# A precedence offset for the small products of scans, sample steps and mixer chunks in a two-layer hybrid trunk

## The chip, the core and the metric

The kernel runs on one core of a Trainium2 chip. The core has engines that run beside each other, each with a queue that it works off in order: TensorE (PE in the profile, with PEld for its weight loads) for products, VectorE (DVE) and ScalarE (ACT) for elementwise work, GpSimd (POOL) for slower elementwise work, and SyncE (SP), from which all large DMA transfers are issued. An instruction waits at the head of its queue for the semaphores of those whose results or buffers it needs. The metric is the device time of one execution in microseconds.

## The reference: one step of a hybrid trunk

1024 prompt tokens and 8 sample tokens go through two layers of width 1024 in fp32. Layer 0 mixes with a Mamba-2 state space scan (SSD, 16 heads) beside an mLSTM (4 heads); layer 1 with RWKV-7 (16 heads of 64). Each mixer is followed by a SwiGLU feed forward of width 2816. For the sample tokens the recurrent states are inputs. The core, cut:

```python
def _trunk(x, conv, ssm, mc, mn, mm, shift, wkv, p):
    for layer in range(DEPTH):
        xn = _rms(x, p['norm_mix'][layer])
        if layer % 2 == 0:
            mix, st = _ssd_mlstm_mixer(xn, conv[i], ssm[i], mc[i], mn[i], mm[i], p, i)
        else:
            mix, st = _rwkv7_mixer(xn, shift[j], wkv[j], p, j)
        x = x + mix.astype(x.dtype)
        x = x + _swiglu(_rms(x, p['norm_ffn'][layer]), p['ffn_w_gate_up'][layer], p['ffn_w_down'][layer])
    y = _rms(x, p['norm_final'])

def _rwkv7_scan(r, decay, k, v, kk, a, s0):
    def step(s, inp):
        r_t, w_t, k_t, v_t, kk_t, a_t = inp
        sa = jnp.einsum('bhvk,bhk->bhv', s, -kk_t)
        s = (s * w_t[:, :, None, :] + sa[..., None] * (kk_t * a_t)[:, :, None, :]
             + v_t[..., None] * k_t[:, :, None, :])
        return s, jnp.einsum('bhvk,bhk->bhv', s, r_t)
```

## The kernel before

**Dense products.** [...] `dense_tile` makes one output tile of 128 rows from 8 or 16 terms into one PSUM bank, `wload` brings 512 KB of weights and splits them on ACT (`whi`, L174) and DVE (`wlo`, L144). Tokens are worked on in two halves (512 prompt tokens; 512 and the 8 sample tokens) from layer 0's output projection on. Dense products are named by their bank: `ps_wo` (RWKV's output projection), `ps_g`, `ps_u` and `ps_d` (the feed forward's gate, up and down products), `ps_rw` (RWKV's projections). `norm_sum` adds squares on DVE (`n_acc`) and sums them over channels by one product (`n_ps`, L211).

**Small products.** The recurrences run beside dense tiles, driven by hooks that advance a generator by a step for each tile of a feed forward or a projection. Beside layer 0's first feed forward half, `ml_decode` steps the mLSTM states of the 8 sample tokens: load `Cs` (L772), update it on DVE (L147), multiply it with the queries (`nums`, L786). The RWKV scan (`rwkv_scan`) runs over the 8 head pairs of a half, numbered 0 to 7; the second half's scan runs beside the end of the second half's projection, the out-projection of the first half and layer 1's feed forward of the first half. For each pair:

- `rw_pre` makes the products `AB` (L1271), four groups of two chunks, and writes the triangular blocks out by DMA;
- `rw_inv` loads them as 32 blocks of 32 x 32 (`X`), sets their diagonals (L1307), inverts them on POOL by 30 dependent pairs of multiply and add (`t`, `X`, L144), writes them (L1317) and loads them into `obd` (L1325), which DVE transposes in blocks (L1327); the first product `off` (L1330) goes through ACT to the second (L1337), whose result goes out by DMA and comes back as `tbd`;
- `rw_front` makes, for each of four groups, the transposes `av` (L1376) and the products `sc`, `Z`, `M` (all issued at L1353), each on a result of the one before that went through DVE;
- `rw_fin` carries the state from chunk to chunk: products `fin` (L1413, L1415), a copy on ACT, a transpose (L1423), a copy on DVE;
- `rw_ln` normalises (`sum2`, L162 and L163, as for `bon` and `kks`); `rw_dec` steps the sample tokens' states (`sav` at L162 and L163, `ysd` at L1533).

The inverse of pair j + 1 is worked on while pair j is scanned.

**What sets the order.** The program is written as one sequence, and a scheduler with a model of the engines' times puts each engine's instructions in the order in which it issues them: among those that are ready by its model, the one of highest precedence, which by default is the earlier one in the program. That order is fixed when the kernel is built; on the chip each queue runs strictly in it. PSUM banks come from pools: three for dense tiles, five or two for the scan's `bank`, two for `pbank`, one for `fin`.

Of the kernel before, what the change touches and what calls it, by code (L numbers as in the profile page):

```python
# [8 lines left out]
F32 = mybir.dt.float32  # L9
# [19 lines left out]
NEG = -1e30  # L29

# [59 lines left out]
def _body(tc, nc, I, O, top):  # L90
# [13 lines left out]
    # two streams of dense products, each with its own weight buffers and banks  # L104
# [28 lines left out]
    ident = cst("ident")  # L133
    S.copy(onesr, cst("onesblk"))
# [24 lines left out]
    def sum2(ps, c, src, hi, lo, e=None):  # L159
        # product with a constant matrix that F32R holds exactly  # L160
        split(src, hi, lo, e)
        PE.matmul(out=ps, lhsT=c, rhs=hi, start=True, stop=False)  # L162
        PE.matmul(out=ps, lhsT=c, rhs=lo, start=False, stop=True)  # L163
# [24 lines left out]
    def dense_tile(w, xs, name, evac, m=128, blocks=NBLK, base=0, th=TA_):  # L188
        # w: list of (hi, lo) per contraction tile; xs: matching (hi, lo) tiles whose column 0 is token base
# [10 lines left out]
    def norm_sum(src, tp, n0, n, w, bank):  # L200
        # Ln of the mean square per token
# [33 lines left out]
    # ------------------------------------------------------------------ layer 0 mixer  # L235
# [37 lines left out]
    # projections with the causal convolution  # L273
# [82 lines left out]
    # gates: rows dt 0..15, i 32..35, f 64..67  # L356
    with gst2:
# [22 lines left out]
        # SSD step sizes and decays  # L380
# [18 lines left out]
        # decode step sizes and decays, per head  # L399
# [11 lines left out]
        # mLSTM row recurrences  # L411
# [25 lines left out]
        # decode gates of the mLSTM  # L437
# [17 lines left out]
    # SSD over chunks  # L455
# [4 lines left out]
    def ssd_chunk(c):  # L460
# [6 lines left out]
        for hf in range(2):  # L467
            b = bank("xT")
            for q in range(4):
                PE.transpose(b[:, q * 128:q * 128 + 128], xc[:, hf * 4 + q, :], ident)  # L470
# [5 lines left out]
        for g in range(2):  # L476
            PE.transpose(b[:, g * 128:g * 128 + 128], bc[:, g, :], ident)
        S.copy(btok, b[:, 0:256])
        xw = sp.tile([128, 1024], F32, name=f"xw{c}", tag="xw", bufs=1)
        for g in range(2):  # L480
# [13 lines left out]
            PE.matmul(out=sc[:, 0:128], lhsT=bc[:, g, :], rhs=bc[:, 2 + g, :], start=True, stop=True)  # L494
            tt(D, D, sc[:, 0:128].unsqueeze(1).to_broadcast([128, 8, 128]))
            yb = bank("yb")
            for q in range(4):
                for h2 in range(2):
                    h = g * 8 + 2 * q + h2
                    PE.matmul(out=yb[h2 * 64:h2 * 64 + 64, q * 128:q * 128 + 128], lhsT=xdt[:, h * 64:h * 64 + 64],  # L500
# [5 lines left out]
            if c > 0:  # L506
                yi = bank("yi")
                for q in range(4):
                    PE.matmul(out=yi[:, q * 128:q * 128 + 128], lhsT=state[g][:, q * 128:q * 128 + 128],
# [12 lines left out]
            PE.matmul(out=su, lhsT=btok[:, g * 128:g * 128 + 128], rhs=xw[:, g * 512:g * 512 + 512],  # L522
# [14 lines left out]
    def ssd_dec_prep():  # L537
# [3 lines left out]
        for i in range(4):  # L541
            PE.transpose(b[0:8, i * 128:i * 128 + 128], bcs[:, i, :], ident)
# [43 lines left out]
    # mLSTM projections  # L586
# [1219 lines left out]
```

## Time and profile before

| | us |
|---|---|
| median of three runs | 3507.38 |
| lowest and highest | 3503.52, 3516.32 |
| span of the profiled execution | 3519.2 |
| TensorE busy in it | 3257.4 (93%) |
| mean granted TensorE clock in it | 0.969 of full speed |

Of the profiled execution the profile has the span, from its first to its last instruction; its time is taken as that. It is 11.8 us above the median of the three timed runs. The profile counts 22615 TensorE instruction records: a small fp32 product makes two of them, one of the dense products one. A view by waits lists, for an engine's instruction, whose end it waited for: total us, times, the longest. A view by windows lists each engine's busy time in a stretch and the clock that TensorE was granted. A row of the timeline has the start, the duration, engine, line, operation, output from inputs, and in brackets how long the engine had sat idle and what ended it. The chain that ended last is followed back from the last instruction to whatever released each step.

### The profile page before, as it was taken

To read this page: it belongs to the slowest core of one execution; us is meant where nothing else is said; L and a number is where in the kernel's file an instruction comes from. 1 tells how busy PE (TensorE), PEld (TensorE's weight loads), DVE (VectorE), ACT (ScalarE), POOL (GpSimd) and SP (SyncE) were. 2 spreads that over 40 slices of the span, in tenths; PEclk is the share of its full clock that TensorE was granted. 3 is DMA by queue.
4 is the path that set the end of the run, shared out by engine and by line. 5 is a ranking of instruction groups with operands and counts; after the bars stand their busy time and mean duration, and the time that the engine had idled before them with its cause. 6 is when DMAs were issued, how large, how long until landed. Compare 5 with 4: busy or idle time off the path is not lost.

```text
span 3519.2 us, 61254 instructions
## 1 busy us (share of the span) xinstructions
PE 3257.4 (93%) x22615; PEld 2997.6 (85%) x22615; DVE 2340.3 (67%) x4315; ACT 1654.6 (47%) x3701; POOL 1237.7 (35%) x1586
## 2 busy tenths in 40 slices
PE   6998899999999999999999968988989999999998
PEld 6987789887778887779999958977888889999998
DVE  8865644466666477676766687667887786575555
ACT  5444435434244245554554555665555554453223
POOL 3257421121200002254645566237686773000000
PEclk9999999999999999999999989998999999999999
DMA  3567674563663243553333324462433333433232
GB/s 117 122 183 215 202 203 143 178 209 126 216 207 108 94 145 109 175 156 93 104 105 97 96 76 134 129 200 76 116 98 98 102 93 90 143 97 97 85 101 68
DMA packets 399135, 458.26 MB, mean 130 GB/s; under 512 B 154756, under 2 KB 295524, under 8 KB 398708
## 3 DMA queue, kind: packets, MB, share of 16 engines
q1 hardware_dynamic: 398836, 454.34, 43.3%
q8 instruction: 179, 2.93, 0.3%
q14 instruction: 120, 0.98, 0.1%
HBM read 352.10 MB, written 102.07 MB: 129 GB/s over the span
## 4 chain that ended last, share of the span: by engine, by line
PE 54%; POOL 13%; DVE 12%; DMA 10%; ACT 5%; issue 4%; SPq 2%; DVEq 0%; ACTq 0%; POOLq 0%
PE ps_g L185 9%; PE ps_u L185 9%; PE ps_d L185 9%; PE ps_rw L185 6%; POOL t L144 5%; POOL X L144 5%; PE ps_in L185 4%; PE ps_out L185 4%; PE ps_o L185 2%; ACT L153 2%; PE ps_wo L185 1%; PE ps_z L185 1%; DVE lp L147 1%; DMA D<-scr_acr 1%; PE cu L726 1%
## 5 line engine op out<-in xcount | busy, mean ns | idle before, releaser
L185 PE MATMUL ps_d<-al,dhi 128*128 128x260 f32 (+2 forms) x1248 | 389.4, 312 | 25.6 <-DVE xc L144 10.3
L185 PE MATMUL ps_d<-ah,dlo 128*128 128x260 f32 (+2 forms) x1248 | 375.6, 301 | 0.0
L185 PE MATMUL ps_d<-ah,dhi 128*128 128x260 f32 (+2 forms) x1248 | 375.3, 301 | 0.0
L144 POOL TENSOR_TENSOR X<-X,t 32x30 f32<-32x30 f32 (+14 forms) x480 | 305.8, 637 | 32.4
L144 POOL TENSOR_TENSOR t<-X 32x30 f32<-32x30 f32 (+14 forms) x480 | 295.5, 616 | 31.0
L185 PEld LDWEIGHTS ps_d<-al,dhi 128*128 128x128 f32 x1248 | 239.4, 192 | 48.3 <-DVE xc L144 15.6
L185 PEld LDWEIGHTS ps_d<-ah,dlo 128*128 128x128 f32 x1248 | 239.8, 192 | 7.9
L185 PEld LDWEIGHTS ps_d<-ah,dhi 128*128 128x128 f32 x1248 | 239.5, 192 | 7.5 <-issue 0.2
L144 DVE TENSOR_TENSOR wlo_g<-raw_g,whi_g 128x512 fp32r<-128x512 f32 (+1 forms) x192 | 143.6, 750 | 113.5 <-ACT whi_g L174 110.8
L942 ACT CAST dhi<-rawd 128x1024 fp32r<-128x1024 f32 x88 | 88.4, 1045 | 210.4 <-PE ps_d L185 205.5
L174 ACT CAST whi_g<-raw_g 128x512 fp32r<-128x512 f32 (+1 forms) x192 | 114.0, 599 | 140.8 <-DMA raw_g<-in_wgu 96.7
L153 ACT ACT_TABLE_LOAD x136 | 174.5, 1283 | 6.2 <-DVE ss L144 3.9
L144 DVE TENSOR_TENSOR wlo_u<-raw_u,whi_u 128x512 fp32r<-128x512 f32 x176 | 137.9, 785 | 56.5 <-ACT whi_u L174 56.0
L174 ACT CAST whi_u<-raw_u 128x512 fp32r<-128x512 f32 x176 | 108.2, 620 | 124.8 <-PE ps_u L185 96.9
L185 PE MATMUL ps_in<-xnl,whi_in 128*128 128x344 f32 x480 | 156.7, 327 | 1.8 <-ACT ext L282 1.8
L185 PE MATMUL ps_in<-xnh,whi_in 128*128 128x344 f32 x480 | 156.2, 325 | 0.0
L185 PE MATMUL ps_in<-xnh,wlo_in 128*128 128x344 f32 x480 | 155.7, 324 | 0.0
L144 DVE TENSOR_TENSOR dlo<-rawd,dhi 128x512 fp32r<-128x512 f32 x176 | 126.2, 770 | 14.7 <-ACT dhi L942 14.7
L144 POOL TENSOR_TENSOR xx<-xa 128x512 f32<-128x512 f32 x8 | 9.7, 1243 | 348.5 <-PE ps_out L185 348.5
L144 POOL TENSOR_TENSOR Bb<-Bc,consts 128x256 f32<-128x256 f32 x64 | 52.6, 823 | 224.3 <-PE M L1353 151.0
L156 ACT CAST ah<-sg 128x260 fp32r<-128x260 f32 (+2 forms) x155 | 67.5, 436 | 134.0 <-DVE sg L147 132.0
L144 DVE TENSOR_TENSOR wlo_rw<-raw_rw,whi_rw 128x512 fp32r<-128x512 f32 x96 | 74.7, 785 | 83.0 <-ACT whi_rw L174 81.9
(959 smaller groups left out, 11939.5 us busy)
## 6 DMA issues: line engine op xcount, KB each, us to landing
raw_g<-in_wgu SPq DMA_DIRECT2D x88, 512.0 KB
raw_u<-in_wgu SPq DMA_DIRECT2D x88, 512.0 KB
rawd<-in_wdn SPq DMA_DIRECT2D x88, 512.0 KB
raw_rw<-in_wrw SPq DMA_DIRECT2D x48, 512.0 KB
raw_o<-in_wout SPq DMA_DIRECT2D x32, 512.0 KB
raw_in<-in_win SPq DMA_DIRECT2D x20, 512.0 KB
D<-scr_acr SPq DMA_DIRECT2D x16, 512.0 KB
Cs<-in_mc SPq DMA_DIRECT2D x16, 512.0 KB
```

Of the source, the lines that this page charges most:

```text
L144: (e or V).tensor_tensor(out=out, in0=a, in1=b, op=op)
L147: (e or V).scalar_tensor_tensor(out=out, in0=a, scalar=s, in1=b, op0=op0, op1=op1)
L153: S.activation(out, a, f, **kw)
L156: S.copy(hi, src)
L174: S.copy(hi[0:p, 0:m], raw[0:p, c0:c0 + m])
L185: PE.matmul(out=ps, lhsT=w[a], rhs=x[b], start=i == 0, stop=i == n - 1)
L726: PE.matmul(out=o, lhsT=ktok[:, (2 * h + k) * 128:(2 * h + k) * 128 + 128], rhs=vw[:, h, :], start=True, stop=True)
L942: S.copy(hi, raw)
```

## The change

Two numbers and a class are added. `Later` issues a product or transpose inside a context that lowers its precedence by an offset: as if it stood 30 instructions further back in the program than it does. The small products are then issued through `PS` (RWKV scan, `sum2`, sample step of the scan) or `PM` (SSD and mLSTM chunks, `qkv` tiles, sample step of the mLSTM) where they were issued through `PE`. The dense products, the norm's product, the gates' transposes and everything on the other engines keep their precedence. No instruction is added, taken away or altered. Comments and blank lines go, so line numbers after the class are 17 higher, and small products are all recorded at the class's two lines (L144 and L148).

```diff
+LATE_SCAN = 30
+LATE_MIX = 30
...
+    class Later:
+
+        def __init__(self, by):
+            self.by = by
+
+        def matmul(self, **kw):
+            with tc.high_priority(offset=-self.by):
+                PE.matmul(**kw)
+
+        def transpose(self, *a):
+            with tc.high_priority(offset=-self.by):
+                PE.transpose(*a)
+
+    PS, PM = Later(LATE_SCAN), Later(LATE_MIX)
...
     def sum2(ps, c, src, hi, lo, e=None):
         split(src, hi, lo, e)
-        PE.matmul(out=ps, lhsT=c, rhs=hi, start=True, stop=False)
-        PE.matmul(out=ps, lhsT=c, rhs=lo, start=False, stop=True)
+        PS.matmul(out=ps, lhsT=c, rhs=hi, start=True, stop=False)
+        PS.matmul(out=ps, lhsT=c, rhs=lo, start=False, stop=True)
...
-                    PE.matmul(out=b[32 * h:32 * h + 32, 0:257], lhsT=qm[:, 2 * h + k, :], rhs=both[h // 2][:, h % 2, k, :],
+                    PM.matmul(out=b[32 * h:32 * h + 32, 0:257], lhsT=qm[:, 2 * h + k, :], rhs=both[h // 2][:, h % 2, k, :],
...
-                PE.matmul(out=b[:, q * 128:q * 128 + 128], lhsT=abp[:, q, :], rhs=d.BK[:, 2 * g + q, :],
+                PS.matmul(out=b[:, q * 128:q * 128 + 128], lhsT=abp[:, q, :], rhs=d.BK[:, 2 * g + q, :],
...
-            PE.matmul(out=b[p4[q], 0:128], lhsT=A[:, q, :], rhs=obd[:, q, :], start=True, stop=True)
+            PS.matmul(out=b[p4[q], 0:128], lhsT=A[:, q, :], rhs=obd[:, q, :], start=True, stop=True)
...
-                PE.matmul(out=b[:, o + q * 128:o + q * 128 + 128], lhsT=lhs(q), rhs=rhs(q), start=True, stop=True)
+                PS.matmul(out=b[:, o + q * 128:o + q * 128 + 128], lhsT=lhs(q), rhs=rhs(q), start=True, stop=True)
...
-            PE.matmul(out=o, lhsT=av[:, 2 + q, :], rhs=DK[:, q, :], start=True, stop=first)
+            PS.matmul(out=o, lhsT=av[:, 2 + q, :], rhs=DK[:, q, :], start=True, stop=first)
```

The same replacement stands at all other small products: the chunk products and transposes of SSD, `qkv` and mLSTM, the second `off`, `av`, the second `fin` and its transpose, and those of the sample steps.

What the change does to the queues shows in the two orders as they are built. **First place**, TensorE, the end of RWKV's out-projection of the first half. Each output tile of it (`ps_wo07_0`, the first 256 tokens of the last tile) has 24 products of 256 columns (`yg0h` and `yg0l` are the high and low parts of its input); `off_24342` is the first product of the inverse of pair 0 of the second scan. Before, it stands behind all 24 and three of the next tile:

```order
L185 MATMUL ps_wo07_0_25612<-yg0l7_25143,whi_wo07512_25608 128x256
L185 MATMUL ps_wo07_0_25612<-yg0h7_25142,wlo_wo07512_25609 128x256
L185 MATMUL ps_wo07_0_25612<-yg0h7_25142,whi_wo07512_25608 128x256
L185 MATMUL ps_wo07_256_25638<-yg0l0_25129,whi_wo070_25604 128x256
L185 MATMUL ps_wo07_256_25638<-yg0h0_25128,wlo_wo070_25605 128x256
L185 MATMUL ps_wo07_256_25638<-yg0h0_25128,whi_wo070_25604 128x256
L1330 MATMUL off_24342<-obd_13757,oa10_24335 32x128 x4
L185 MATMUL ps_wo07_256_25638<-yg0l1_25131,whi_wo070_25604 128x256
```

and with the change behind the first six:

```order
L202 MATMUL ps_wo07_0_25612<-yg0l0_25129,whi_wo070_25604 128x256
L202 MATMUL ps_wo07_0_25612<-yg0h0_25128,wlo_wo070_25605 128x256
L202 MATMUL ps_wo07_0_25612<-yg0h0_25128,whi_wo070_25604 128x256
L202 MATMUL ps_wo07_0_25612<-yg0l1_25131,whi_wo070_25604 128x256
L202 MATMUL ps_wo07_0_25612<-yg0h1_25130,wlo_wo070_25605 128x256
L202 MATMUL ps_wo07_0_25612<-yg0h1_25130,whi_wo070_25604 128x256
L144 MATMUL off_24342<-obd_13757,oa10_24335 32x128 x4
L202 MATMUL ps_wo07_0_25612<-yg0l2_25133,whi_wo070_25604 128x256
```

The `off` product has moved ahead of 21 dense products. **Second place**, DVE at the same point of the program: `xc0` are the residual sums of that projection, `wlo_g10` the split of the feed forward's first weights, `obd` the transpose on which `off` waits. Before:

```order
L144 TENSOR_TENSOR xc0_6_25126<-xc0_6_25126,ps_wo06_0_25550 128x256
L144 TENSOR_TENSOR n_acc_25719<-n_acc_25719,n_sq_25736 128x256
L144 TENSOR_TENSOR wlo_g10_00_25840<-raw_g10_0_25837,whi_g10_00_25839 128x512
L1327 STREAM_TRANSPOSE obd_13757<-obd_13757 128x512
L144 TENSOR_TENSOR xc0_6_25126<-xc0_6_25126,ps_wo06_256_25576 128x256
L144 TENSOR_TENSOR wlo_g10_0512_25844<-raw_g10_0_25837,whi_g10_0512_25843 128x512
```

and with the change:

```order
L161 TENSOR_TENSOR xc0_6_25126<-xc0_6_25126,ps_wo06_0_25550 128x256
L1344 STREAM_TRANSPOSE obd_13757<-obd_13757 128x512
L161 TENSOR_TENSOR n_acc_25719<-n_acc_25719,n_sq_25736 128x256
L161 TENSOR_TENSOR wlo_g10_00_25840<-raw_g10_0_25837,whi_g10_00_25839 128x512
L161 TENSOR_TENSOR xc0_6_25126<-xc0_6_25126,ps_wo06_256_25576 128x256
L161 TENSOR_TENSOR wlo_g10_0512_25844<-raw_g10_0_25837,whi_g10_0512_25843 128x512
```

The transpose has moved ahead of one sum of squares and one weight split. **Third place**, TensorE in layer 0's feed forward of the first half, beside which the mLSTM's sample step runs: `ps_d004_0` to `ps_d004_7` are down products of 512 columns, six to a tile, and `nums_8618` is the product of the fifth request. Before, it stands behind tile 3:

```order
L185 MATMUL ps_d004_3_0_8479<-ah00_3_8243,dlo003_8342 128x512
L185 MATMUL ps_d004_3_0_8479<-ah00_3_8243,dhi003_8341 128x512
L786 MATMUL nums_8618<-Cs40_8600,qm0_7921 32x257 x2
L185 MATMUL ps_d004_4_0_8487<-al00_2_8071,dhi002_8334 128x512
L185 MATMUL ps_d004_4_0_8487<-ah00_2_8070,dlo002_8335 128x512
```

and with the change behind tile 5:

```order
L202 MATMUL ps_d004_5_0_8495<-ah00_3_8243,dlo003_8342 128x512
L202 MATMUL ps_d004_5_0_8495<-ah00_3_8243,dhi003_8341 128x512
L144 MATMUL nums_8618<-Cs40_8600,qm0_7921 32x257 x2
L202 MATMUL ps_d004_6_0_8503<-al00_2_8071,dhi002_8334 128x512
L202 MATMUL ps_d004_6_0_8503<-ah00_2_8070,dlo002_8335 128x512
```

It has moved behind 12 more dense products; the product of the fourth request (`nums_8445`) has moved from ahead of tile 0 to behind tile 1, 12 products as well.

More of the change, by code (lines that the diff above doesn't have):

```diff
@@ L476, in ssd_chunk @@
         for g in range(2):
-            PE.transpose(b[:, g * 128:g * 128 + 128], bc[:, g, :], ident)
+            PM.transpose(b[:, g * 128:g * 128 + 128], bc[:, g, :], ident)
         S.copy(btok, b[:, 0:256])
@@ L493, in ssd_chunk @@
             sc = bank("cb")
-            PE.matmul(out=sc[:, 0:128], lhsT=bc[:, g, :], rhs=bc[:, 2 + g, :], start=True, stop=True)
+            PM.matmul(out=sc[:, 0:128], lhsT=bc[:, g, :], rhs=bc[:, 2 + g, :], start=True, stop=True)
             tt(D, D, sc[:, 0:128].unsqueeze(1).to_broadcast([128, 8, 128]))
@@ L594, in qkv_tile @@
                 b = bank("qk")
-                PE.matmul(out=b[:, 0:n], lhsT=wq[:, j, :], rhs=a[:, n0:n0 + n], start=True, stop=True)
+                PM.matmul(out=b[:, 0:n], lhsT=wq[:, j, :], rhs=a[:, n0:n0 + n], start=True, stop=True)
                 act(sg[:, n0:n0 + n], b[:, 0:n], AF.Copy, scale=1.0 if j == 0 else 1.0 / 16)
@@ L703, in ml_chunk @@
             o = b[:, 0:257]
[L704 removed]
+            PM.matmul(out=o, lhsT=Dm[:, h, :], rhs=va[:, h, :], start=True, stop=c == 0)
             if c > 0:
                 for k in range(2):
[L707 removed]
+                    PM.matmul(out=o, lhsT=qc[:, 2 * h + k, :], rhs=Cst[:, h, k, :], start=False, stop=k == 1)
             act(dn[:, h:h + 1], b[:, 256:257], AF.Abs)
@@ L1336, in rw_inv @@
         for u in range(4):
-            PE.matmul(out=b[p4[u], 0:128], lhsT=U[:, p4[u]], rhs=obd[:, u, :], start=True, stop=True)
+            PS.matmul(out=b[p4[u], 0:128], lhsT=U[:, p4[u]], rhs=obd[:, u, :], start=True, stop=True)
         S.copy(fl(A), b[:, 0:128])
@@ L1412, in rw_fin @@
             o = b[:, 0:128]
-            PE.matmul(out=o, lhsT=av[:, 2 + q, :], rhs=DK[:, q, :], start=True, stop=first)
+            PS.matmul(out=o, lhsT=av[:, 2 + q, :], rhs=DK[:, q, :], start=True, stop=first)
             if not first:
-                PE.matmul(out=o, lhsT=d.ST, rhs=rM[:, q, :], start=False, stop=True)
+                PS.matmul(out=o, lhsT=d.ST, rhs=rM[:, q, :], start=False, stop=True)
             sb = R_.sbd
@@ L1422, in rw_fin @@
             if not last:
-                PE.transpose(b[:, 128:256], sb, ident)
+                PS.transpose(b[:, 128:256], sb, ident)
                 d.ST = gpl.tile([128, 128], F32, name=f"ST{nm}{c}", tag="ST")
@@ L1476, in rw_dec_prep @@
         b = pbank("kksd")
-        PE.matmul(out=b[:, 0:64], lhsT=onesr.bitcast(F32), rhs=f2(sq), start=True, stop=True)
+        PS.matmul(out=b[:, 0:64], lhsT=onesr.bitcast(F32), rhs=f2(sq), start=True, stop=True)
         ts(f2(sq), b[:, 0:64], 1e-24, ALU.max)
@@ L1491, in rw_dec_prep @@
         b = pbank("bond")
-        PE.matmul(out=b[:, 0:64], lhsT=onesr.bitcast(F32), rhs=f2(k), start=True, stop=True)
+        PS.matmul(out=b[:, 0:64], lhsT=onesr.bitcast(F32), rhs=f2(k), start=True, stop=True)
         d.bon = k
@@ L1541, in rw_dec_out @@
         b = pbank("ycd")
-        PE.matmul(out=b[:, 0:64], lhsT=centr.bitcast(F32), rhs=y, start=True, stop=True)
+        PS.matmul(out=b[:, 0:64], lhsT=centr.bitcast(F32), rhs=y, start=True, stop=True)
         act(rv, b[:, 0:64], AF.Square)
@@ L1545, in rw_dec_out @@
         b = pbank("yvd")
-        PE.matmul(out=b[:, 0:64], lhsT=onesr.bitcast(F32), rhs=rv, start=True, stop=True)
+        PS.matmul(out=b[:, 0:64], lhsT=onesr.bitcast(F32), rhs=rv, start=True, stop=True)
         act(rv, b[:, 0:64], AF.Ln, bias=R_.lneps, scale=1.0 / 64)
```

30 lines of the change are left out of this document (14 added, 16 removed).

## The prediction

> **What bounds the kernel now.** The page comes first: the span, the busy shares, the chain that ended last.
>
> ```profile
> span 3519.2 us, 61254 instructions
> PE 3257.4 (93%) x22615; PEld 2997.6 (85%) x22615; DVE 2340.3 (67%) x4315; ACT 1654.6 (47%) x3701; POOL 1237.7 (35%) x1586
> PE 54%; POOL 13%; DVE 12%; DMA 10%; ACT 5%; issue 4%; SPq 2%; DVEq 0%; ACTq 0%; POOLq 0%
> ```
>
> TensorE (PE) is busy 93% of the span and holds 54% of the chain; POOL has 35% of the busy time, yet 13% of the chain. A change of order alone can win at most what PE idles, 3519.2 - 3257.4 = 262 us, and what it runs at half clock. No instruction is added or removed here, so every term below is a wait that goes, comes or moves.
>
> The second view is the order of the two programs, engine by engine, for it says where anything can differ at all. It differs in four stretches only: in the first half of layer 0's feed forward, at the start of the first RWKV scan, for some 50 us inside the second half's RWKV projection, and from the out-projection through the first half of layer 1's feed forward, beside which the second scan runs. All chunks of SSD and mLSTM, all of qkv, both second halves of the feed forward and the tail stand row by row as they did. The third view, busy time by stretches of time, gives those four their size (columns: stretch, length, busy PE, weight loads, DVE, ACT, POOL, granted clock, DMA share, GB/s); the fifth row is 34 us in which PE never waited.
>
> ```profile
> 896.00:1017.00 121.00, 117.84 (x543) 88.11 (x542) 80.58 (x133) 35.93 (x59) 19.36 (x16) 0.97 0.59 193
> 1573.00:1593.00 20.00, 18.13 (x132) 16.74 (x131) 16.70 (x34) 8.80 (x12) 10.64 (x21) 0.91 0.27 74
> 2094.00:2143.00 49.00, 40.47 (x313) 38.05 (x312) 43.78 (x92) 30.56 (x93) 27.92 (x43) 0.93 0.28 65
> 2412.00:3021.00 609.00, 547.56 (x4531) 521.87 (x4530) 454.81 (x882) 326.73 (x802) 389.45 (x581) 0.96 0.36 98
> 2378.00:2412.00 34.00, 34.00 (x290) 33.91 (x289) 25.89 (x43) 14.58 (x33) 31.12 (x41) 1.00 0.37 108
> ```
>
> The first three hold 121 + 20 + 49 = 190 us, with 3.2 + 1.9 + 8.5 = 13.6 us of idle PE. The fourth holds 609 us with 609 - 547.56 = 61.4 us of it: this is where the change is decided. The fifth row gives the pitch with which I turn places into time: 34.00 / 290 = 0.117 us for each PE row of the trace. What PE waited for in the fourth stretch (us in total, times, longest):
>
> ```profile
> PE ps_d L185 <- DVE xc L144: 9.1, 12, 2.3
> PE off L1330 <- DVE obd L1327: 8.2, 3, 5.0
> PE ps_g L185 <- DVE f10l L144: 5.3, 5, 2.1
> PE n_ps L211 <- DVE n_acc L144: 4.5, 1, 4.5
> PE sav L162 <- ACT dh L156: 4.2, 3, 3.5
> PE Z L1353 <- DMA tbd<-scr_toff: 3.8, 2, 2.3
> PE off L1337 <- DMA obd<-scr_tblk: 3.7, 4, 1.6
> PE M L1353 <- DVE Z L1388: 3.4, 3, 2.1
> PE fin L1413 <- DVE y L1428: 3.4, 5, 1.2
> PE Z L1353 <- DVE RD L144: 3.2, 3, 1.3
> PE sc L1353 <- DVE RD L144: 3.1, 4, 1.2
> PE fin L1413 <- DVE RD L144: 2.4, 1, 2.4
> PE fin L1423 <- ACT sbd L1419: 1.6, 3, 0.8
> PE AB L1271 <- DVE BK L144: 1.2, 2, 0.6
> ```
>
> Three kinds are to be seen. The steps of the scan (Z, M, fin, sc, AB) waited 3.8 + 3.2 + 3.4 + 3.4 + 2.4 + 1.6 + 3.1 + 1.2 = 22.1 us for results just made. The two products of a pair's inverse (off) waited 8.2 + 3.7 = 11.9 us at the end of a long chain through POOL. The dense products waited 9.1 + 5.3 us, with the norm product n_ps 4.5, and the change does not name them.
>
> **The change part by part.** Of 2911 small products 878 stand elsewhere among the dense ones, and 659 of these 878 stand EARLIER, not later, by 6 to 16 dense products on average for most of the scan's kinds. The last product of the scan stands 30 dense products earlier, 30 x 0.117 = 3.5 us.
>
> *The first three stretches.* Layer 0's sample step waits once:
>
> ```profile
> PE nums L786 <- DVE Cs L147: 3.1, 1, 3.1
> 911.11 0.93 SPq L772 DMA_DIRECT2D Cs<-in_mc  x2
> 918.26 1.42 DVE L147 SCALAR_TENSOR_TENSOR Cs<-Cs,mg_bc,tv 128x512 f32<-128x512 f32 x2 [4.04 <-DMA Cs<-in_mc]
> ```
>
> The product that waited (nums_8618) stands 12 dense products later, at 117.84 / 543 = 0.217 us each 2.6 us of cover. But SP issues the load that it needs only when the step before it (nums_8445) is done, and that stands 12 products later as well; behind Cs on DVE now stand three operations less. The chain moves with the cover: 0, between -3.1 (all of the wait) and +2.6 (the load later, the cover used up).
>
> ```profile
> PE kks L163 <- POOL sql L144: 1.3, 1, 1.3
> ```
>
> The start of the first scan waited 1.3 us here, and dense products now stand before it: -1, between -1.3 and 0. In the third stretch DVE is busy 43.8 of 49 us against PE's 40.5, so PE's order does not set its length: 0, within 2 either way.
>
> *The end of the out-projection.* Here off_24342 stands after 6 of the 24 products of ps_wo07_0 where it stood after 24 + 3, so 21 x 0.117 = 2.5 us earlier. Its operand is not earlier:
>
> ```profile
> 2419.49 0.71 DVE L1327 STREAM_TRANSPOSE obd<-obd 128x512 f32<-128x512 f32 x1 [7.33 <-DMA obd<-scr_tblk]
> ```
>
> DVE had been idle 7.33 us for a DMA, so its transpose, two places further ahead in DVE's queue, starts when it did. PE's wait of 5.0 us (the longest of off L1330) becomes 7.5, and all dense products behind it, the residual sums on DVE that need them and the n_ps product come 2.5 us later: **+2.5**, between +0.9 (if the 21 products then cover the 1.6 us that the second off product waited for) and +4.0 (if the sum of squares n_acc and the weight split wlo, now behind the transpose on DVE and estimated at its 0.71 us each, add to the wait of n_ps).
>
> *The second off product of each pair.* Between the two off products of a pair the order has 5.1 to 5.4 us of work (quartiles, at 0.117 us a row) where it had 4.1 to 5.2. It waited 3.7 us in four places: **-3**, between -3.7 and 0.
>
> *The scan's steps.* From each small product to the next that needs it I counted the PE rows between. The median cover goes from 2.78 to 2.59 us for sc to Z, from 2.63 to 2.79 for Z to M, from 2.43 to 2.35 for fin to its transpose, from 2.6 to 2.4 for AB to AB. The links are about as far apart as they were: **0**. Bounds: half of the 22.1 us goes, or comes again, 11 either way.
>
> *The inverse chain.* A pair's last AB product goes through DMA to POOL, which inverts for 50 to 60 us; DMA and a transpose lead to the first off product. Relative to the off product of the pair before, the last AB stands earlier by 5.2 us for pair 2 and 4.5 for pair 7, and later by 7.7, 9.9, 5.6 and 3.5 us for pairs 3 to 6 (pairs are numbered 0 to 7; counted in both orders at 0.117 us a row). These are the last AB products and the start of the inverse (MEMSET) for those four, with pair 4's transpose and first off product:
>
> ```profile
> 2553.29 0.61 PE L1271 MATMUL AB<-BK,abp 128*128 128x128 f32 x4
> 2576.76 0.15 POOL L1307 MEMSET X<- 32x32 f32 x1 [1.38 <-DMA X<-scr_ablk]
> 2636.93 0.61 PE L1271 MATMUL AB<-BK,abp 128*128 128x128 f32 x4
> 2654.25 0.15 POOL L1307 MEMSET X<- 32x32 f32 x1 [1.69 <-DMA X<-scr_ablk]
> 2720.56 0.71 DVE L1327 STREAM_TRANSPOSE obd<-obd 128x512 f32<-128x512 f32 x1
> 2723.78 0.43 PE L1330 MATMUL off<-obd,oa 128*32 128x128 f32 x8
> 2702.24 0.61 PE L1271 MATMUL AB<-BK,abp 128*128 128x128 f32 x4
> 2724.79 0.15 POOL L1307 MEMSET X<- 32x32 f32 x1 [1.39 <-issue]
> 2783.47 0.61 PE L1271 MATMUL AB<-BK,abp 128*128 128x128 f32 x4
> 2794.06 0.15 POOL L1307 MEMSET X<- 32x32 f32 x1 [4.40 <-issue]
> ```
>
> From the end of AB to POOL's start it took 22.9, 16.7, 21.9 and 10.0 us. The shortest, 10.0, is what the way costs; so AB can come 12.9, 6.7, 11.9 and 0 us later before POOL does. Pairs 3 and 5 hide their 7.7 and 5.6; pair 4 is late by 9.9 - 6.7 = 3.2, pair 6 by 3.5. Pair 4's off product had stood ready for 2723.78 - 2721.27 = 2.5 us before PE took it, pair 6's for 0.1: what reaches PE is 0.7 + 3.4 = **+4**. Bounds: 0 (the earlier pairs 2 and 7 give it back) and 22, the slower rival below.
>
> *The clock.* Number of stalls over 2 us about as before: **0**, within 3.
>
> Sum: 0 - 1 + 0 + 2.5 - 3 + 0 + 4 + 0 = +2.5 us. On the profiled execution that is 3519.2 + 2.5 = 3521.7. That execution lies 11.8 us over the median of the three runs, 3507.38; the difference carries over, which gives **3510 us**.
>
> **The rivals.** What a measurement of this kernel can tell from no change is about 0.5%, 17.5 us.
>
> *Faster: the scan's waits go.* "Later" could set scan products behind dense ones, so that results are ready when PE reaches them. That would take half to all of the 22.1 us, and what follows a stall:
>
> ```profile
> 2569.91 0.43 PE L1330 MATMUL off<-obd,oa 128*32 128x128 f32 x8 [2.44 <-DVE obd L1327]
> 2570.45:2573.85 3.40, 3.40 (x17) 3.40 (x17) 1.35 (x5) 1.09 (x4) 1.34 (x2) 0.51 0.20 39
> sum 44.30, PE 38.24 PEld 35.62 DVE 34.05 ACT 25.67 POOL 26.99; mean PE 4.78 PEld 4.45 DVE 4.26 ACT 3.21 POOL 3.37
> ```
>
> Behind a stall of 2.44 us PE ran 3.4 us at a granted clock of 0.51. The last row is the sum over the eight such windows of the fourth stretch, 44.3 us, which cost about 22 us; without the first two, 3.4 and 13.7 us behind the waits of 5.0 and 4.5 us, there are 27.2 us behind stalls of single small products, which cost 13.6. Half of 22.1 + 13.6 is 18, with the 1 + 3 us of the sum above 22: 3507 - 22 = **3485**. Against it: most of the moved products stand earlier, and the covers counted above are as long as before. [...]
>
> *Slower: the inverse chain decides.* The slack that pairs 3 and 5 show is not free time of the way alone: POOL did another operation just before. If POOL's other work is late with the scan that feeds it, all four delays reach the off products: 7.7 + 9.9 + 5.6 + 3.5 = 26.7 us, less the 2.5 us for which pair 4's off product had stood ready and 0.5, 1.5 and 0.1 for the others (the same two views), 22; four stalls over 2.4 us bring four windows of 3.4 us at half clock, 4 x 1.7 = 7; with +2.5 - 3 - 1 the sum is +27: **3534**. It decides once the way from AB to POOL's start is above about 10 us in all four pairs. For it: POOL's 13% of the chain. Against it: waits of this kind overlap, since a late PE gives POOL time for the next pair.
>
> *The change does not do what it says.* No chunk of SSD, qkv or mLSTM moves, and 659 of 878 moved products go forward. That speaks for no change of the time, and lies within the forecast.
>
> **How the numbers follow.** Chance 0.61 for the forecast, 3510, with its own range of 3495 to 3526 (the scan's steps 11 either way, the other bounds partly with them); 0.21 for the faster rival; 0.18 for the slower. The range of 3485 to 3533 takes in the forecast's own, half of the faster and half of the slower case. Faster by over 0.5% is below 3489.8, slower above 3524.9: nearly the rivals alone, so 0.21, 0.61, 0.18.
>
> **What would show it.** The three stretches before 2378 us should keep their length within 3 us, and the one from 2412 us its 609 within 15. In that one the wait of the first off product at the out-projection should be near 7.5 us where it was 5.0, the second off products should wait under 1 us in sum, Z, M, fin, sc and AB about 22. The sum of off's waits for obd is the test between forecast (about 8.2 + 2.5 + 4 = 15) and slower rival (over 30); the granted clock of 0.96 there should hold, and 0.98 or more would speak for the faster one. The forecast is wrong if the scan's steps lose more than half of their waits or gain as much, or if a stretch whose order is the same row by row changes its length by more than 5 us.

## The result, and the profile after

The changed kernel is slower: 3537.16 us median of four runs (3534.11 to 3538.07) beside 3510.11 us for the kernel before, a ratio of 1.0065 with a 95% interval of 1.0051 to 1.0079, or +22.8 us (the two medians themselves are 27.1 us apart, 1.0077, within the interval). That is 3530 us on the median that the prediction used. The profiled execution has a span of 3532.3 us, 13.1 us more than the one of before (that one was among the slower of its kind; a second trace of the same order, below, has 3508.5).

The head of the page after, to be read beside the page before:

```profile
span 3532.3 us, 61254 instructions
PE 3269.2 (93%) x22615; PEld 3007.2 (85%) x22615; DVE 2330.2 (66%) x4315; ACT 1653.5 (47%) x3701; POOL 1229.9 (35%) x1586
PE 59%; DVE 12%; POOL 10%; DMA 8%; ACT 5%; issue 4%; SPq 2%; DVEq 0%; ACTq 0%; POOLq 0%
```

The instructions are the same in number, and TensorE (PE) is busy 11.8 us longer with them: idle time did not grow as much as the span, the same products took longer. POOL's share of the chain fell from 13% to 10%, which speaks against the inverse chain as what grew.

Which stretch, and by what? The next two fences are the view by windows, of before and of after, between the same instructions of both programs: from the first gate tile of layer 1's feed forward (`ps_g10_0`) to the first gate block of its second half (`ps_g11_0_512`) in the last row, from the third tile of the out-projection (`ps_wo02`) to that gate tile in the row above, and two earlier stretches in the first rows (`ps_u00_4` to `ps_g00_6`, and `ps_rw110` to `ps_wo02`). Columns as in the prediction.

```profile
903.10:940.90 37.80, 34.64 (x154) 24.98 (x153) 29.72 (x43) 7.21 (x11) 15.28 (x12) 0.91 0.72 243
2113.20:2381.40 268.20, 245.59 (x1811) 229.38 (x1811) 172.85 (x318) 165.97 (x413) 116.96 (x154) 0.94 0.51 154
2381.40:2436.20 54.80, 42.53 (x343) 40.14 (x341) 35.44 (x64) 25.50 (x60) 42.22 (x67) 0.92 0.37 104
2436.20:3120.90 684.70, 631.35 (x5215) 605.41 (x5215) 506.52 (x1003) 364.06 (x869) 376.75 (x553) 0.97 0.35 99
```

```profile
902.40:940.50 38.10, 34.72 (x161) 24.77 (x159) 26.64 (x41) 7.78 (x12) 14.14 (x12) 0.91 0.71 240
2111.50:2374.40 262.90, 242.48 (x1813) 227.19 (x1812) 173.30 (x316) 165.69 (x411) 116.18 (x154) 0.95 0.52 157
2374.40:2435.30 60.90, 47.17 (x355) 44.58 (x353) 38.03 (x69) 28.08 (x62) 43.51 (x71) 0.86 0.34 93
2435.30:3134.00 698.70, 645.28 (x5201) 618.40 (x5199) 496.08 (x995) 360.74 (x867) 368.60 (x549) 0.95 0.34 97
```

The last two rows hold the loss: 6.1 and 14.0 us. In the last row PE was idle 684.7 - 631.35 = 53.4 us before and 698.7 - 645.28 = 53.4 us after: in this pair of traces the waits have the same sum. What differs is the granted clock, 0.97 to 0.95 there and 0.92 to 0.86 in the row above. The waits themselves changed places (PE's waits of after in that last stretch, the longest groups):

```profile
PE ps_d L202 <- DVE xc L161: 8.2, 7, 2.4
PE fin L144 <- DVE y L1445: 6.3, 3, 2.8
PE sav L144 <- DVE wlo_u L161: 4.8, 1, 4.8
PE ps_u L202 <- DVE sg L164: 4.2, 2, 2.9
PE ps_g L202 <- DVE f10l L161: 3.5, 3, 1.4
PE Z L144 <- DVE RD L161: 3.0, 2, 1.9
PE yv L144 <- POOL y L161: 2.5, 1, 2.5
PE off L144 <- DVE obd L1344: 2.5, 2, 1.6
```

One of them shows the price. Around the wait of `sav`, 4.8 us (windows of 3.4, 10.2 and 3.4 us):

```profile
2674.40:2677.80 3.40, 0.50 (x1) 0.19 (x1) 3.40 (x5) 1.13 (x3) 3.17 (x5) 1.00 0.73 219
2677.80:2688.00 10.20, 7.50 (x43) 7.26 (x44) 10.04 (x15) 6.53 (x12) 8.13 (x9) 0.50 0.34 99
2688.00:2691.40 3.40, 3.40 (x31) 3.40 (x31) 3.11 (x6) 2.40 (x7) 3.17 (x5) 0.99 0.21 68
```

PE is idle 2.9 us in the first window, and the clock is 0.50 for the three windows behind it. Half of the length of such windows, summed from `ps_wo02` to `ps_g11_0_512`, is called the half-clock loss here. It is 23.9 us in the trace of before and 42.7 us in that of after, 18.8 us more, where the span between these two instructions grew by 20.2 us. The sum also counts windows in which PE idles, as it did for 2.7 of the 10.2 us above, time that the waits have already; counted only while PE was busy, it is 20.6 and 37.1 us, 16.4 us more.

### The profile page after: what moved, and what is told of

The parts are those of the page before. It is cut to its first block, busy times and chain, and to the rows that moved or that the text cites. A ratio compares the mean times of both kernels' runs of the same rounds, so it can differ in the third digit from the quotient of the medians.

```text
span 3532.3 us, 61254 instructions
## 1 busy us (share of the span) xinstructions
PE 3269.2 (93%) x22615; PEld 3007.2 (85%) x22615; DVE 2330.2 (66%) x4315; ACT 1653.5 (47%) x3701; POOL 1229.9 (35%) x1586
## 4 chain that ended last, share of the span: by engine, by line
PE 59%; DVE 12%; POOL 10%; DMA 8%; ACT 5%; issue 4%; SPq 2%; DVEq 0%; ACTq 0%; POOLq 0%
PE ps_g L202 11%; PE ps_u L202 10%; PE ps_d L202 9%; PE ps_rw L202 6%; PE ps_in L202 4%; POOL t L161 4%; POOL X L161 4%; PE ps_out L202 3%; PE ps_o L202 2%; ACT L170 2%; PE ps_wo L202 1%; PE fin L144 1%; PE M L144 1%; PE ps_z L202 1%; PE sc L144 1%
## 5 line engine op out<-in xcount | busy, mean ns | idle before, releaser
L202 PE MATMUL ps_d<-al,dhi 128*128 128x260 f32 (+2 forms) x1248 | 389.2, 312 | 22.8 <-DVE xc L161 8.2
```

The source lines that it names most:

```text
L202: PE.matmul(out=ps, lhsT=w[a], rhs=x[b], start=i == 0, stop=i == n - 1)
```

## The experiments

Two theories were put against each other. **S**: the scan's products lose because they are set later. **K**: the order of the second scan is new from end to end, whatever is set later; the waits bunch in other places, and TensorE's clock makes the time of it. The prediction's slower rival, the **inverse chain**, was the third.

**First four runs: parts of the change, and a second trace of both orders.** In the second run all that goes through `PS` goes back to `PE`, in the third all that goes through `PM`, in the fourth `AB` and both `off` alone; in the control everything does. One line of each kind:

```diff
-        PS.matmul(out=ps, lhsT=c, rhs=hi, start=True, stop=False)
+        PE.matmul(out=ps, lhsT=c, rhs=hi, start=True, stop=False)
...
-                    PM.matmul(out=b[32 * h:32 * h + 32, 0:257], lhsT=qm[:, 2 * h + k, :], rhs=both[h // 2][:, h % 2, k, :],
+                    PE.matmul(out=b[32 * h:32 * h + 32, 0:257], lhsT=qm[:, 2 * h + k, :], rhs=both[h // 2][:, h % 2, k, :],
...
-            PS.matmul(out=b[p4[q], 0:128], lhsT=A[:, q, :], rhs=obd[:, q, :], start=True, stop=True)
+            PE.matmul(out=b[p4[q], 0:128], lhsT=A[:, q, :], rhs=obd[:, q, :], start=True, stop=True)
```

The control:

> Every small product is issued at its own precedence again, with the class still in the file; the order of every engine is that of the kernel before, row by row. A control, and a second trace of that order. All theories: 0 within 5 us of the kernel before. It tells how far the half-clock time of TensorE between the out-projection and the end of the first half's last feed forward (22.2 us lost before, 41.0 after) changes from one execution to another: the theory that the clock makes the loss needs this control below 30 us.

Layer 0's part alone:

> Later for chunk products, qkv and the mLSTM's sample step only; the scan and its sums at their own precedence. The order changes from the sample step on and once more in the second scan, 464 places where the whole change has 478. Theory K (any new order of the second scan changes how TensorE's waits bunch, and the half-clock windows behind them make the time): clearly different from before although no product of the scan is set later, between -10 and +25 us, and equal within 6 us to what the trace shows of lost clock and waits in that stretch. Theory S (the scan's products lose because they are set later): 0 within 6 us.

The scan's part alone:

> Later for the scan, its sums and the scan's sample step only; nothing of layer 0 is set later. Its order in the second scan differs from before in 330 places and from the whole change in 448. Theory S: slower by the whole +24 us. Theory K: some other number between -10 and +25 us, with the difference in lost clock between the out-projection and the feed forward's end equal to it within 8 us.

The whole without the inverse chain's products:

> The whole change, but AB and both off products of the inverse chain at their own precedence. The order that comes out is that of the whole change, row by row on TensorE: setting these products later moved nothing. So +24 us within 5 for all theories; a second trace of the changed order. Theory K: lost clock in the stretch of the second scan 35 us or more again, off's waits for the transpose again below 10 us in sum. The inverse-chain rival of the prediction would want those waits above 30 us.

Measured, as ratios with intervals: control 1.0005 (0.9992 to 1.0019), layer 0's part alone 1.0029 (1.0017 to 1.0042), the scan's part alone 1.0023 (1.0012 to 1.0033), the whole without `AB` and `off` 1.0059 (1.0039 to 1.0078). The stretches in their traces, in us, cut at the first products of the tiles named (the first two columns have one order, the next two another):

| from, to | before | control | whole | without AB, off | layer 0 alone | scan alone |
|---|---|---|---|---|---|---|
| start, ps_u00_4 | 903.1 | 898.1 | 902.4 | 906.1 | 906.8 | 901.5 |
| ps_u00_4, ps_g00_6 | 37.7 | 37.5 | 38.1 | 38.0 | 40.8 | 38.3 |
| ps_g00_6, ps_rw110 | 1172.3 | 1170.9 | 1171.0 | 1171.7 | 1169.5 | 1174.1 |
| ps_rw110, ps_wo02 | 268.2 | 266.0 | 262.9 | 262.0 | 263.3 | 264.9 |
| ps_wo02, ps_g10_0 | 54.7 | 54.9 | 60.9 | 59.5 | 59.0 | 54.4 |
| ps_g10_0, ps_g11_0_512 | 684.7 | 682.3 | 698.7 | 697.3 | 686.9 | 688.4 |
| ps_g11_0_512, end | 398.3 | 398.6 | 398.3 | 398.5 | 398.9 | 398.5 |
| half-clock loss, ps_wo02 to ps_g11_0_512 | 23.9 | 27.3 | 42.7 | 35.8 | 37.5 | 25.6 |
| of it while PE was busy | 20.6 | 23.6 | 37.1 | 30.5 | 31.8 | 22.4 |
| PE idle there | 65.6 | 63.0 | 67.2 | 69.0 | 62.3 | 60.7 |

The order decides where time goes: both traces of an order agree within 3 us in every stretch but the first. In that one PE's order is the same in all six up to the last 9 us or so, and the time to that place moves from 885.5 to 892.4 us all the same. From `ps_wo02` to `ps_g11_0_512` the mean of the two traces goes from 738.3 to 758.2 us, +19.9; half-clock loss goes from 25.6 to 39.2, +13.6, of which +11.7 while PE was busy (22.1 to 33.8), and idle time from 64.3 to 68.1, +3.8. The clock is some three fifths of the loss, waits a fifth; 4.4 us, in which PE was busy longer than its half clock accounts for, stay without a name. The expectation for the control, half-clock loss below 30, held, and 35.8 held the bound of 35 barely (the 22.2 and 41.0 in that expectation are of a slightly different stretch).

S fell in part with the second and the third run: no product of the scan is set later in the second, and it loses 10 us (0.0029 x 3510); the scan's part alone loses 8 us, where S wanted the whole 24. Layer 0's part alone has the whole change's 59 us at the end of the out-projection, and the scan's part alone has before's 54. So the +5.4 us there come with layer 0's part, which runs some 1500 us earlier, and not through any precedence of the scan; the way that is left is the scheduler's model, which orders the rest by the times that it reckons with. The inverse chain fell with the fourth: the order with `AB` and `off` at their own precedence is the same, and the waits of `off` are small in all (PE's waits for off, of the control and of the whole change, `ps_wo02` to `ps_g11_0_512`):

```profile
PE off L1347 <- DVE obd L1344: 8.0, 4, 5.3
PE off L1354 <- DMA obd<-scr_tblk: 4.9, 3, 3.1
```

```profile
PE off L144 <- DMA tbd<-scr_tblk: 5.5, 1, 5.5
PE off L144 <- DVE obd L1344: 2.5, 2, 1.6
```

They went from 13 us to 8. K's second claim, that the time lost equals lost clock and waits, held for most of the whole change (11.7 + 3.8 = 15.5 of 19.9 us) and for layer 0 alone (+9.7 us of clock while PE was busy and -2.0 of idle time against +7.6 in that part). It failed for the scan alone: 0.3 and -3.6 against +4.4, so PE was busy 7.7 us longer there than its half clock accounts for, and why stays open.

**Four runs on the place at the out-projection, on filling a wait, and on the sign.** In the fifth run products of constants fill the norm product's wait, in the sixth (on the kernel before) and the seventh (on the whole change) they push the first `off` behind all dense products of the out-projection, 21 further than before; the eighth sets all small products earlier:

```diff
         ps = bank("n_ps")
+        if fill_at[0] and n0 == 0:
+            for _ in range(56):
+                PE.matmul(out=ps[:, 0:128], lhsT=onesr, rhs=centr, start=True, stop=True)
...
         b = bank("off")
+        if hf == 1 and j == 0:
+            for _ in range(24):
+                PE.matmul(out=b[:, 0:128], lhsT=onesr, rhs=centr, start=True, stop=True)
...
-LATE_SCAN = 30
-LATE_MIX = 30
+LATE_SCAN = -30
+LATE_MIX = -30
```

> The kernel before, and 56 products of two constant matrices (128 columns each, estimated at 0.06 us from the 0.235 us of a product with 512 columns: 3.4 us) are put into the norm's own PSUM bank ahead of the norm product that waits 4.5 us at the end of the out-projection. They take no wait away and add work; everything up to there has the order of before. Theory K (idle time in a window of 3.4 us halves the clock of the next): the three windows at half clock behind that wait go or become one, the stretch from the third tile of the out-projection to the first tile of the feed forward stays at 55 us or falls to 52, and the two tiles behind it, 50 us, lose 2 to 3 us less clock. A theory of waits alone: the stretch becomes 0 to 3 us longer and the clock stays. What follows is ordered anew, within 15 us either way.

> The kernel before, and 24 products of constants (1.4 us) are put into the bank of the first off product of pair 0 of the second scan ahead of it; with them it stands behind all products of the last tile of the out-projection, 24 dense products later than before and 45 later than with the change. Step of the prediction tested: at this place a wait of 5.0 us (before) or 7.5 (change) comes from off standing ahead of dense work. If so, the wait falls below 2.5 us and the stretch to the first tile of the feed forward from 54.8 us to 50 to 53. If the wait only moves to the norm product or to off's second product, the stretch stays at 54 to 57.

> The whole change, with the same addition: off of pair 0 stands behind the last dense product of the out-projection, 45 products later than with the change. The stretch of 60.9 and 59.5 us in two traces of the changed order should fall by 5 to 9 us, to 52 to 55. The order of the rest of the second scan comes out anew. Theory S (setting the scan's products later loses by itself, 14 us in the feed forward): 12 to 18 us slower than before in all. Theory K: anything from -8 to +20, with clock lost and waits of the trace summing to it within 8 us.

> The opposite sign: all small products get a precedence 30 places earlier in place of later. Orders of SSD, qkv and mLSTM chunks move too (rows 928 to 4504 of TensorE). Theory S (later is what loses): 10 to 25 us faster than before, or at least not slower. Theory K (any new order of the scan's part loses against one that was picked because it ran well, by lost clock and bunched waits): 5 to 30 us slower.

The fifth missed. It is 1.0035 (1.0021 to 1.0049), and the stretch became 62.9 us, 8 more. The fill was dearer than estimated: 20 such products took 2.36 us, 0.118 each, so 56 are 6.6 us of work (its timeline: start, length, the fill, and the off behind it),

```profile
2417.19 2.43 PE L232 MATMUL n_ps<-centr,onesr 128*128 128x128 f32 x20
2419.55 0.42 PE L1361 MATMUL off<-obd,ou 128*32 128x128 f32 x8
```

and a new wait (`bond`, 2.8 us) came into the middle of it. The next stretch of two tiles did lose less clock, 1.7 us where it was 5.7, but the run cannot tell clock from waits, since work, order and waits all changed.

The sixth missed too: 1.0012 (1.0001 to 1.0022), stretch 57.0, and `off` waited 7.4 us although 21 more dense products stood ahead of it (the 24 added products themselves came to stand 130 us earlier, in the projection, which changed the order from there on). The transpose that it waits for came 43.5 us after `ps_wo02`'s start where it comes 38 in the kernel before; PE had reached the out-projection earlier (the projection, `ps_rw110` to `ps_wo02`, took 259.8 us where it was 268.2 and 266.0), and the chain through POOL had not. At this place it mattered less where `off` stands than when its operand comes out of the chain through POOL. The seventh hit its stretch, 54.5 us, and is 1.0043 (1.0028 to 1.0058), 15 us slower, within both theories: its half-clock loss while PE was busy is 37.2 us, as in the first trace of the whole change, though the stretch at the out-projection is as short as before.

In the eighth, with all small products 30 places *earlier*, the kernel is 1.0069 (1.0055 to 1.0082), as slow as with 30 later. S expected it faster. It is no mirror image of the change, though: from `ps_wo02` to `ps_g11_0_512` its trace is only 4.4 us above the mean of before, and 10 us lie between `ps_g00_6` and `ps_rw110` (1181.8 us).

**The clock by itself.** The ninth run is a kernel of its own, with bursts of products and waits of set lengths:

```diff
+    def burst(n, sec):
+        ps = pp.tile([128, 256], F32, name=f"b{sec}", tag="b")
+        for i in range(n):
+            PE.matmul(out=ps, lhsT=w, rhs=y[0] if i == 0 else x, start=i == 0, stop=i == n - 1)
...
+PLAN = [(30, [(48, 0)]), (30, [(48, 2)]), (30, [(48, 4)]), (30, [(48, 6)]), (30, [(48, 8)]), (30, [(48, 12)]),
+        (30, [(48, 16)]), (30, [(48, 20)]),
+        (30, [(88, 4), (8, 4)])]
```

> Computes nothing of the reference (all outputs zero but one): nine sections, each 30 times a burst of 48 dense products of 256 columns (5.6 us) and a wait of TensorE for a chain of DVE operations on that burst's result, of 2, 4, 6, 8, 10, 14, 18 and 22 operations; the ninth section has bursts of 88 and of 8 products by turns, with a wait of the third section's kind behind each, so that two waits come within about 2.5 us. It measures what a wait does to the clock by itself. Theory K (the granted clock is halved for 3.4 us when TensorE idled more than about half of the 3.4 us ahead, as the traces so far have it: from full clock, idle under 1.6 us was followed by half clock in 16 of some 1990 windows, over 1.8 us in 45 of 47): sections with waits up to 1.6 us keep a granted clock over 0.97, sections with waits of 2 to 3 us fall to 0.75 or below; the ninth falls below the third although each of its waits is as long. A theory in which only a wait over 3.4 us costs clock: all sections with waits under 3.4 us at 0.97 or more, and the ninth like the third.

Its nine sections (view by windows):

```profile
3.49:203.83 200.34, 181.29 (x1440) 176.05 (x1441) 21.18 (x89) 0.00 (x0) 0.00 (x0) 1.00 0.34 106
203.83:416.15 212.32, 179.42 (x1440) 174.21 (x1441) 33.17 (x150) 0.00 (x0) 0.00 (x0) 1.00 0.00 1
416.15:642.16 226.01, 179.31 (x1440) 174.09 (x1441) 45.00 (x210) 0.00 (x0) 0.00 (x0) 1.00 0.00 1
642.16:907.37 265.21, 204.80 (x1440) 199.59 (x1441) 56.56 (x270) 0.00 (x0) 0.00 (x0) 0.89 0.00 1
907.37:1198.27 290.90, 216.75 (x1440) 211.54 (x1441) 68.27 (x330) 0.00 (x0) 0.00 (x0) 0.85 0.00 1
1198.27:1530.65 332.38, 230.73 (x1441) 225.52 (x1441) 91.63 (x450) 0.00 (x0) 0.00 (x0) 0.81 0.00 1
1530.65:1899.07 368.42, 239.27 (x1440) 234.06 (x1441) 115.03 (x570) 0.00 (x0) 0.00 (x0) 0.78 0.00 1
1899.07:2309.24 410.17, 253.50 (x1440) 248.30 (x1441) 138.43 (x690) 0.00 (x0) 0.00 (x0) 0.75 0.00 1
2309.24:2799.38 490.14, 398.39 (x2880) 387.87 (x2880) 88.22 (x413) 0.00 (x0) 0.00 (x0) 0.90 0.00 1
```

The waits between the bursts are 0.64, 1.10, 1.56, 2.01, 2.47, 3.39, 4.31 and 5.22 us. Up to 1.56 us they cost themselves and nothing else, the clock is 1.00. Behind each wait of 2.01 us the same 48 products take (204.80 - 179.31) / 30 = 0.85 us longer, behind waits of 2.47 us 1.2, of 5.22 us 2.5. The ninth section has 60 waits of 1.55 us, which cost no clock in the third; here two stand close together, and for each pair the products take (398.39 - 2 x 179.31) / 30 = 1.3 us longer. **The same waits, bunched, cost more than their sum.** The figure of 0.75 or below for 2 to 3 us was too low: the clock is 0.89 in the section with waits of 2.01 us and 0.85 in that of 2.47 us, where a burst, 5.98 us at full clock (179.31 / 30), takes no more than those 0.85 and 1.2 us longer.

Counted over windows of 3.413 us, on whose borders all 73 and 79 changes of the clock in the traces of before and after lie (idle time of PE in a window, and how many of the next windows were at half clock; of the ninth run without windows that were idle throughout):

```
from full clock:       idle under 1.6 us   1.6 to 1.8    over 1.8 us
  before and after         9 of 1827        5 of 18       61 of 63
  ninth run                0 of 442         6 of 12       97 of 100
from half clock:       idle under 0.6 us                  over 0.6 us
  before and after         6 of 81                         50 of 50
  ninth run                0 of 150                        67 of 67
```

(The expectation above gave two of these counts as 16 of 1990 and 45 of 47; recounted, they are 9 of 1827 and 61 of 63.) So in these runs a window in which PE idled over 1.8 of the 3.413 us was followed by half clock in 158 of 163 cases, and at half clock one with over 0.6 us of it was followed by half clock again in all 117. Idle time is not all: what the nine windows with less than 1.6 us have besides was not found.

**Offsets, and the smallest change of order.** The last three runs take 5 and 60 in place of 30, and, with everything else back at `PE`, later for the two `off` products alone:

```diff
-LATE_SCAN = 30
-LATE_MIX = 30
+LATE_SCAN = 5
+LATE_MIX = 5
...
+            PS.matmul(out=b[p4[q], 0:128], lhsT=A[:, q, :], rhs=obd[:, q, :], start=True, stop=True)
...
+            PS.matmul(out=b[p4[u], 0:128], lhsT=U[:, p4[u]], rhs=obd[:, u, :], start=True, stop=True)
```

> The whole change with 5 in place of 30 as the offset. Theory S (lateness loses, in proportion): 0 to 5 us slower than before. Theory K: at the end of the out-projection the first off product stands where it stands with 30 (behind 7 products of the last tile), so the stretch there is 59 to 61 us, +5; the second scan behind it is ordered anew, so +5 to +25 us in all.

> The whole change with 60 as the offset. Theory S: 35 to 50 us slower than before. Theory K: the first off product stands 57 rows ahead of the last tile of the out-projection, 63 ahead of its place with 30, so 63 x 0.117 = 7 us more of wait: stretch 65 to 68 us; orders of SSD and mLSTM chunks and of the first scan move as well; +5 to +35 us in all, no multiple of the whole change's 23.

> Later for the two off products alone, nothing else. One small product of pair 4's second off stands two rows later than before (at about 2740 us); all that follows up to the scan's end is ordered anew, in 187 places. Theory S: 0 within 4 us, since almost nothing is later. Theory K: the part from the eleventh gate tile on, 388 us in two traces of before, changes by up to 15 us either way, and nothing ahead of it changes.

Offset 5 is 1.0017 (1.0003 to 1.0032), +6 us, which does not part the theories; its stretch at the out-projection was 60.5 us, as expected, but the feed forward behind it 685.2 us, as before. Offset 60 is 1.0088 (1.0072 to 1.0105), +31 us, where S expected 35 to 50 and K 5 to 35. The place was wrong there: the stretch from `ps_wo02` is 56.3 us, not 65 to 68, and `off` waits 3.3 us. Most of the loss lies ahead of it, in the first scan and the projection: 12.5 us from `ps_d012_1` to `ps_rw110` (550.8 where it was 538.3) and 17 to 19 us from there to `ps_wo02` (285.5 us). With -30, 5, 30 and 60 the losses are 24, 6, 23 and 31 us. Among the later offsets the loss grows, as S has it, though not in proportion and not in the same places; what speaks against S is the loss at -30, with layer 0's part alone, and in the last run.

The last run is the smallest change. Its order is that of the kernel before up to the second `off` of pair 4, of which three of four products move behind the two transposes `av`. What follows, up to the scan's end, is ordered anew in 187 places (the expectation's count), and the kernel is 1.0043 (1.0028 to 1.0057), 15 us slower; S expected 0 within 4. From `ps_g10_0` to `ps_g10_10` the trace has 295.3 us beside the control's 295.2; from `ps_g10_10` to `ps_g10_14` 143.9 beside 132.5. The last run's rows and the control's:

```profile
2427.90:2723.20 295.30, 266.99 (x2179) 254.28 (x2179) 235.41 (x451) 168.59 (x415) 209.40 (x308) 0.95 0.36 97
2723.20:2867.10 143.90, 123.86 (x987) 117.61 (x985) 103.26 (x199) 74.31 (x187) 100.12 (x149) 0.93 0.34 88
```

```profile
2427.60:2722.80 295.20, 266.74 (x2180) 254.53 (x2180) 233.13 (x451) 168.59 (x415) 208.29 (x308) 0.96 0.36 97
2722.80:2855.30 132.50, 119.62 (x995) 114.30 (x994) 103.92 (x197) 75.38 (x189) 101.81 (x149) 0.96 0.37 100
```

Idle time is 20.0 against 12.9 us, 7.1 us of waits, and PE is busy 123.86 against 119.62 us, 4.2 us longer at a clock of 0.93 against 0.96. Here the waits are the larger part. The traced execution took 3519.55 us where the median of this kernel is 3533.75, so most of the 15 us stands in no trace. All ten orders that differ from before were slower, by 4 to 31 us (three of them have added products, in the fifth run 6.6 us of work); none beats both kernels. Why the order of before is the best of the eleven stays open: that it had been picked because it ran well, as the eighth expectation has it, is shown by no run.

## Why the prediction was right and wrong

The forecast was 3510 us, no change; the time is 3530 on the same footing, within the stated range of 3485 to 3533, but beyond 0.5% and beyond the forecast's own range of 3495 to 3526. That it lies within the stated range is luck: the range took in half of the slower rival, whose mechanism did not come true, and not what made the time. Of the prediction's own signs, the stretch from 2412 us became 627.0 us where 609 within 15 was allowed, and the granted clock there fell from 0.96 to 0.93. By its steps:

- **What bounds the kernel**: right. All of the loss lies in the fourth stretch, on PE; SSD, mLSTM and the tail kept their times (table above).
- **First three stretches**, forecast 0, -1 and 0: +0.5 us for the first (`nums` waits 3.4 us where it was 3.1, so the chain moved with the cover as argued); the wait of `kks` at the start of the first scan is gone, but `ps_d` waits 1.5 us more. The third, with the projection behind it, gained 4.6 us by the means of two traces each, which was forecast as 0 within 2.
- **The end of the out-projection**, forecast +2.5 as a longer wait: +5.4. The wait hardly grew, 5.0 to 5.5 us, since the transpose came 1.0 us earlier after `ps_wo02`. The loss stands behind it. 21 more products than before follow `off`, and those right behind it run at half clock, 0.21 us each in the timeline in place of 0.117; `Z` now stands ahead of the `n_ps` that waits, and waits itself (rows of after: the off, two of the products behind it, and Z):

```profile
2412.24 0.65 PE L144 MATMUL off<-obd,oa 128*32 128x128 f32 x8 [5.54 <-DMA tbd<-scr_tblk]
...
2413.21 0.42 PE L202 MATMUL ps_wo<-yg0h,wlo_wo 128*128 128x256 f32 x1
2413.42 0.41 PE L202 MATMUL ps_wo<-yg0h,whi_wo 128*128 128x256 f32 x1
...
2426.30 1.19 PE L144 MATMUL Z<-RD,tbd 128*128 128x128 f32 x4 [3.32 <-DMA tbd<-scr_toff]
```

- **The second off product**, forecast -3: its waits fell from 3.7 us (4.9 in the control) to none in the trace of after and 1.0 in the second of that order. Right.
- **The scan's steps**, forecast 0 within 11: Z, M, fin, sc and AB wait 19.9 us in sum after, 23.2 before (from the same views with their smaller rows). Right, and the sum of all waits is as good as unchanged.
- **The inverse chain**, forecast +4: wrong. All waits of `off` together went down by about 5 us, where the test wanted about 15 us for the forecast and over 30 for the slower rival. Later `AB` and `off` are no part of it: without them the order is the same.
- **The clock**, forecast "number of stalls over 2 us about as before: 0, within 3": this is the step that failed. The number of stalls over 2 us from `ps_wo02` to `ps_g11_0_512` did stay, 10 and 8 in the two traces of before, 10 and 9 in those of after, and yet the half-clock loss while PE was busy grew by 11.7 us (means of two traces), some three fifths of the loss in the stretch. The count of long stalls was the wrong quantity. (The price that the faster rival put on its eight windows, half of 44.3 us or about 22, is a little high for the same reason as above: PE was busy for 38.24 us of them, which makes 19.) Idle time within one window of 3.4 us is what goes with half clock in nearly all windows counted above (158 of 163 with over 1.8 us); two short waits add up in it, as the pairs of 1.55 us in the ninth section did (1.3 us a pair), and the sum of the waits says nothing of how they fall. The other theory of the ninth expectation, that only a wait over 3.4 us costs clock, would have given 0 as well, since waits of that length were 3 and 2 before and 3 and 3 after; the ninth run disagrees with it: waits of 2.01 us brought the clock to 0.89.

The slower rival had the size, 3534, and the wrong mechanism, so that its size agrees is luck too. The rival that the change does not do what it says was right in what it says of the order, and wrong in taking that for no change of the time: products that stand earlier instead of later are as much a new order as what was intended.

## What to carry to other kernels

Where a scheduler's model fixes the order, a precedence set in one place can reorder everything behind it, as three products moved in the last run did: compare the whole order first, and treat the time as that of a new draw, not as the sum of the products that were meant to move. Judge an order by how its waits fall together, not by their sum: here waits of 1.55 us cost no clock when they stood alone, and 1.3 us a pair beyond themselves when two stood close together. An experiment that sets one part of such a change tells little of that part until its order has been compared with that of the whole.

## What the runs showed of the hardware

- In the traces of before and after the clock granted to TensorE was 1.00 or 0.50, and all of its 73 and 79 changes lie on a grid of windows of 3.413 us. A window with over 1.8 us of idle time was followed by half clock in 158 of 163 cases (two traces and the ninth run), one with less than 1.6 us in 9 of 2269. At half clock, a window with over 0.6 us of idle time was followed by another in 67 of 67 cases of the ninth run and in 50 of 50 of the traces of before and after.
- The grid lay differently in two executions: the first window begins 0.29 us after the span's start in the trace of before and 1.76 us after it in that of after. One order has a half-clock loss of 35.8 us in one execution and 42.7 us in another, with waits of 69.0 and 67.2 us. That the place of the grid makes this difference, and some of the spread between executions of one kernel (3503 to 3526 us in 29 runs), was not shown.
- A product with 128 columns (the fill of the fifth run) took 0.118 us, as long as a dense product with 256 (0.117 us a row in the prediction's fifth stretch).
